# Keeping the high and low halves of every weight block in an HBM scratch

## The chip, the cores and the metric

The kernel runs on one core of one Trainium2 chip. The metric is the device time of one execution in microseconds (us). Five engines work side by side: TensorE (PE; its weight loads are listed as PEld), VectorE (DVE), ScalarE (ACT), GpSimd (POOL) and SyncE (SP), which here issues every DMA from one in-order queue. They are held together by semaphores.

## The reference

One layer of a hybrid decoder runs over a prompt of 2048 tokens and over 8 sample sequences of 8 tokens, with shared weights and D = 1024. In float32, cut to the order of its steps:

```
h = rmsnorm(x);  u = h @ w_in                     # [conf_val | conf_gate | q k v | z | beta | a]
conf = swish(layernorm(dwconv31(val * sigmoid(gate))))
q, k, v = silu(dwconv4(qkv));  q, k = l2norm(q), l2norm(k)
o = gated_delta_rule(q, k, v, g, beta, S);  o = rmsnorm(o) * silu(z)
x = x + concat(conf, o) @ w_out
gate, val = dwconv3(rmsnorm(x) @ w_up)            # 2 x 2816 columns
x = x + (silu(gate) * val) @ w_down
x = x + (p @ w_ple) * sigmoid(x @ w_ple_gate);  y = rmsnorm(x)
```

The states of the convolutions and of the delta rule are outputs too.

## The kernel before

**Number format.** Every large product is made of float32r operands in halves: `hi` is the operand rounded to float32r, `lo` what is left. `gemm` (L269) sums `hi*hi + hi*lo + lo*hi` in one PSUM bank, three matmuls for each of 8 slices of the inner dimension, so a weight block of 1024 x 128 takes 24 matmuls, of 512 columns or of two chunks (256 and 256, in the last pass 256 and 320).

**Passes and phases.** The prompt is cut into four passes of 512 tokens (L1327); the last one carries the 64 sample tokens too. Each pass runs phase b (`w_in`: beta and a, conformer blocks, k, q, v and z, the inverses of triangular blocks, the scan of the delta rule), phase w (`w_out`, residual, norm; its 8 blocks are gone through twice, once for each chunk of tokens), phase f (`w_up` and `w_down`, 22 columns in 11 pairs: four up blocks of a pair, then the product of the pair before with two `w_down` blocks) and phase l (`w_ple_gate`, last norm, output; the norm of the next pass's x runs inside it). A pass uses 114 weight blocks and the small block of beta and a (`ba_weights`, L1284); 106 of the 114 are different.

**The stream of weights.** The blocks are listed in the order of their use (`stream`, L1293 to L1318). `get` (L257) keeps three of them ready: when a block is taken, the one two further on is started. `wblock` (L247) starts one: SP loads 512 KB into a `raw` tile (three buffers), ACT casts it to `whi` (three buffers), and POOL or DVE, as `lo_e` says, subtracts `wlo = raw - whi` (three buffers). A `whi` or `wlo` buffer comes free when TensorE has read the block three back; a `raw` buffer comes free when its split is done. `w_up` and `w_in` blocks are read in runs of 512 bytes, `w_down` blocks in runs of 4 KB. Every block of every pass is loaded and split anew.

**Around it.** In phase f, ACT empties each PSUM bank of an up product twice (`row`, and `y` with the last tap, L1123 to L1125), DVE adds two more taps (`end`, L1127), ACT and POOL split the product of the halves into `fbuf` (L1174), and for the down product DVE adds each bank to the residual `X` (L1149). Three PSUM banks (`g`) serve all the large products. In phase b DVE does the taps of the convolutions, POOL the taps of conformer block 3 (L44) and then the chain of the inverses: blocks go through HBM (`scr`, L760 to L765), 62 operations on POOL write `Tb` (L772 to L777), they come back through `scr2` into `X`, and POOL copies them to `T` (L833), from which TensorE builds the full inverses. In phase w the residual comes back from its scratch `xT` (L1078), 1 MB in runs of 8 KB.

**What sets the order.** The program is written in dependency order, and a scheduler with its own timing model places the instructions on the engines; stretches marked `high_priority` go first. The order on SP is such an order too: a DMA that waits holds back those behind it.

## Time and profile before

| | before |
|---|---|
| median of 3 runs | 3376.66 us (3370.89 to 3382.05) |
| span of the profiled execution | 3377.1 us |
| TensorE busy | 3045.9 us, 90% |
| DVE, POOL, ACT busy | 2285.6, 1932.9, 1480.6 us |
| POOL `wlo` | 362 of 2429 ns |
| DVE `wlo` | 94 of 1403 ns |
| ACT `whi` | 456 of 1051 ns |
| moved by DMA | 295.34 MB, 87 GB/s |

The profiled execution has its span as its own time; it lies 0.4 us above the median of the runs. Busy shares are means over phases with different limits, so the table of stretches and the waits of a phase say more than the page's first line. A stretch's idle time of TensorE is its length less its busy time. In a list of waits the engine that stood still stands first, then what ended the wait. In the chain of waits each piece is what the end of the program waited for at that time. The granted clock is given as a share of TensorE's full speed: 1.00 is its higher level, 2.4 GHz, and a mean below 1 says that a part of the stretch ran at 1.2 GHz.

### The profile page before, as it was taken

What the parts mean: (1) busy time and instruction counts of PE and PEld (TensorE: products, weight loads), DVE (VectorE), ACT (ScalarE), POOL (GpSimd) and SP (SyncE); (2) the same over time, 40 slices, a digit from 0 to 9 for tenths busy, and PEclk for the clock granted to TensorE, in tenths of its full rate; (3) what the DMA queues carried; (4) which work ended last, traced back from release to release, by engine and by line L of the source; (5) the groups of instructions that cost most, each with busy time, mean ns of one, the idle gap of its engine ahead of it and who ended that gap; (6) DMA issues with size and microseconds to landing.
All of it is one profiled execution on the core that took longest, in us unless ns stands there. A gap on an engine that the chain in (4) does not pass through costs nothing. (4 is left out here: it accounts for less than half of the span.)

```text
span 3377.1 us, 48322 instructions
## 1 busy us (share of the span) xinstructions
PE 3045.9 (90%) x17710; PEld 2682.5 (79%) x17710; DVE 2285.6 (68%) x4306; ACT 1480.6 (44%) x2947; POOL 1932.9 (57%) x1987
## 2 busy tenths in 40 slices
PE   7889899999888899998988889999996988999998
PEld 6668777778767877778866877777986878999998
DVE  6999754457898864447698965445796877554555
ACT  4536443344535443334543544334452335443443
POOL 6972555564982455556694455566486404655552
PEclk8999999999989999999998999999997878999999
DMA  4223332233321433233322433233322123222231
GB/s 127 72 57 105 104 106 89 86 96 105 78 69 42 141 106 91 84 100 94 88 72 50 129 97 100 88 93 95 94 59 69 46 79 116 76 76 83 84 90 60
DMA packets 480596, 295.34 MB, mean 87 GB/s; under 512 B 49674, under 2 KB 462859, under 8 KB 479328
## 3 DMA queue, kind: packets, MB, share of 16 engines
q1 hardware_dynamic: 480359, 292.27, 30.1%
q8 instruction: 139, 2.28, 0.3%
q14 instruction: 98, 0.79, 0.1%
HBM read 269.69 MB, written 22.90 MB: 87 GB/s over the span
## 5 line engine op out<-in xcount | busy, mean ns | idle before, releaser
L93 PE MATMUL g<-hT,whi 128*128 128x512 f32 (+2 forms) x5664 | 1519.9, 356 | 60.9 <-ACT t L112 18.9
L109 POOL TENSOR_TENSOR wlo<-raw,whi 128x1024 fp32r<-128x1024 f32 x362 | 877.6, 2429 | 602.4 <-ACT whi L112 567.9
L93 PEld LDWEIGHTS g<-hT,whi 128*128 128x128 f32 x5664 | 1028.5, 196 | 189.7 <-ACT t L112 21.5
L93 PE MATMUL g<-hT,wlo 128*128 128x512 f32 (+2 forms) x2832 | 1001.2, 355 | 8.7 <-POOL wlo L109 8.6
L100 DVE SCALAR_TENSOR_TENSOR y<-row,ffS,y 128x512 f32<-128x512 f32 x352 | 466.0, 1324 | 605.0 <-ACT y L112 601.5
L112 ACT ACTIVATE whi<-raw 128x1024 fp32r<-128x1024 f32 x456 | 475.0, 1051 | 409.8 <-PE g L93 244.6
L93 PEld LDWEIGHTS g<-hT,wlo 128*128 128x128 f32 x2832 | 555.6, 196 | 70.9 <-POOL wlo L109 10.6
L93 PE MATMUL g<-fbuf,whi 128*128 128x512 f32 (+2 forms) x1760 | 474.7, 359 | 64.5 <-DVE X L109 37.4
L93 PEld LDWEIGHTS g<-fbuf,whi 128*128 128x128 f32 x1760 | 305.2, 189 | 134.1 <-DVE X L109 59.5
L109 DVE TENSOR_TENSOR X<-X,g 128x512 f32<-128x512 f32 (+2 forms) x504 | 280.5, 567 | 134.3 <-PE g L93 132.4
L100 DVE SCALAR_TENSOR_TENSOR cacc<-H,cfS,cacc 128x512 f32<-128x512 f32 x352 | 321.4, 928 | 10.4 <-ACT cacc L112 8.5
L93 PE MATMUL g<-fbuf,wlo 128*128 128x512 f32 (+2 forms) x880 | 305.0, 354 | 0.2 <-POOL wlo L109 0.2
L109 POOL TENSOR_TENSOR cacc<-cacc,pr 128x256 f32<-128x256 f32 x224 | 203.9, 932 | 18.4 <-ACT pr L112 17.2
L93 PE MATMUL g<-mx,whi 128*128 128x256 f32 (+1 forms) x1024 | 201.1, 292 | 3.4 <-ACT mx L112 1.4
L112 ACT ACTIVATE fbuf<-y 128x512 fp32r<-128x512 f32 (+1 forms) x88 | 56.8, 645 | 333.3 <-DVE y L109 333.3
L93 PE MATMUL g<-x,whi 128*128 128x256 f32 (+1 forms) x1024 | 197.0, 289 | 0.0
L93 PEld LDWEIGHTS g<-fbuf,wlo 128*128 128x128 f32 x880 | 165.5, 189 | 21.4 <-POOL wlo L109 0.4
L109 POOL TENSOR_TENSOR fbuf<-y,fbuf 128x512 fp32r<-128x512 f32 (+1 forms) x88 | 118.5, 1347 | 108.8 <-ACT fbuf L112 108.8
L93 PEld LDWEIGHTS g<-mx,whi 128*128 128x128 f32 x1024 | 163.0, 192 | 5.6 <-ACT mx L112 2.1
L112 ACT ACTIVATE row<-g 128x512 f32<-128x512 f32 (+1 forms) x292 | 141.7, 485 | 53.0 <-PE g L93 51.2
L93 PEld LDWEIGHTS g<-x,whi 128*128 128x128 f32 x1024 | 164.1, 193 | 0.4
L112 ACT ACTIVATE pr<-H,cfS 128x256 f32<-128x256 f32 x232 | 114.5, 505 | 102.3 <-POOL cacc L109 100.3
(346 smaller groups left out, 4589.4 us busy)
## 6 DMA issues: line engine op xcount, KB each, us to landing
raw<-in_w_up_dram SPq DMA_DIRECT2D x176, 512.0 KB
raw<-in_w_in_dram SPq DMA_DIRECT2D x96, 512.0 KB
raw<-in_w_down_dram SPq DMA_DIRECT2D x88, 512.0 KB
raw<-in_w_out_dram SPq DMA_DIRECT2D x64, 512.0 KB
raw<-in_w_ple_gate_dram SPq DMA_DIRECT2D x32, 512.0 KB
out_dram<-yt SPq DMA_DIRECT2D x16, 512.0 KB
X<-xT SPq DMA_DIRECT2D x7, 1024.0 KB
xt<-in_x_prompt_dram SPq DMA_DIRECT2D x12, 512.0 KB
```

The costliest lines, as they stand in the source:

```text
L93: T.matmul(out, lhsT=lhsT, rhs=rhs, start=start, stop=stop, skip_group_check=skip)
L100: e.scalar_tensor_tensor(out=out, in0=in0, scalar=scalar, in1=in1, op0=op0, op1=op1)
L109: e.tensor_tensor(out=out, in0=a, in1=b, op=op)
L112: A.activation(out, in_, f, **kw)
```

## The change

The first time a block is used, it is loaded and split as before, now into one tile `w` of 8 KB a partition that holds both halves (three buffers in place of three `whi` and three `wlo`, the same space). SP then stores this tile, 1 MB in runs of 8 KB, to a tile of its own in HBM. Each later use, in passes 2 to 4 and in the second round over `w_out` in pass 1, loads the 1 MB from there straight into `w`, with no `raw` tile, no cast and no subtraction. The block of beta and a is treated alike. The diff, without the comments that it drops:

```diff
+    hw = ctx.enter_context(tc.tile_pool(name="hw", bufs=1, space=DRAM))
...
-    def wblock(src, hi_e="a", lo_e="g"):
-        raw = raw_tile("raw")
-        SY.dma_start(raw, src)
-        hi = wp.tile([P, KD, P], F32R, tag="whi", name=nm("whi"), bufs=3)
-        lo = wp.tile([P, KD, P], F32R, tag="wlo", name=nm("wlo"), bufs=3)
-        split(raw, hi, lo, hi_e, lo_e)
-        return hi, lo
+    halves = {}
+
+    def w_tile():
+        return wp.tile([P, 2, KD, P], F32R, tag="w", name=nm("w"), bufs=3)
+
+    def wblock(key, src, hi_e="a", lo_e="g"):
+        w = w_tile()
+        if key in halves:
+            SY.dma_start(w.bitcast(F32), halves[key])
+        else:
+            raw = raw_tile("raw")
+            SY.dma_start(raw, src)
+            split(raw, w[:, 0], w[:, 1], hi_e, lo_e)
+            halves[key] = hw.tile([P, 2, KD, P], F32, tag=nm("halves"), name=nm("halves"))
+            SY.dma_start(halves[key], w.bitcast(F32))
+        return w[:, 0], w[:, 1]
...
     def ba_weights():
+        if "ba" in halves:
+            w = w_tile()
+            SY.dma_start(w[:, 0].bitcast(F32), halves["ba"])
+            return w[:, 0], None
...
-            push(cols(w_in[0], b * P), lo_e=LO[0] if ip else "g")
+            push_cols("in", w_in[0], b * P, lo_e="g")
```

The other calls of `push` get a key (name and column) in the same way.

**ACT, steady part of phase f, pass 2.** The rows are part of one pair; `fbuf` is the split of a finished column, `whi` the cast of a weight block, `row` and `y` empty a bank. Before:

```order
L112 ACTIVATE whi_2252_12956<-raw_2251_12954 128x1024
L112 ACTIVATE row_2249_12921<-g_2250_12923 128x512
L112 ACTIVATE y_2248_12920<-g_2250_12923,ffS_2905 128x512
L112 ACTIVATE y_2248_12920<-y_2248_12920 128x512
L112 ACTIVATE whi_2258_12998<-raw_2257_12996 128x1024
L112 ACTIVATE row_2255_12961<-g_2256_12963 128x512
L112 ACTIVATE y_2254_12960<-g_2256_12963,ffS_2905 128x512
L112 ACTIVATE fbuf_1912_10721<-y_2254_12960 128x512
```

After:

```order
L113 ACTIVATE row_2174_12831<-g_2175_12833 128x512
L113 ACTIVATE y_2173_12830<-g_2175_12833,ffS_2935 128x512
L113 ACTIVATE y_2173_12830<-y_2173_12830 128x512
L113 ACTIVATE row_2178_12867<-g_2179_12869 128x512
L113 ACTIVATE y_2177_12866<-g_2179_12869,ffS_2935 128x512
L113 ACTIVATE fbuf_1917_10627<-y_2177_12866 128x512
```

The casts ahead of `row` are gone; the rest stands in the same order. ACT has 456 casts of weight blocks before and 106 after.

**SP, start of phase w, pass 2.** `X<-xT` is the residual, `pt` an input of phase l, `raw` a block of `w_out`, `w<-halves` a block from the scratch. Before:

```order
L249 DMA raw_1816_10148<-in_w_out_dram 128x8x128 [waits DMAHW7_49,DMAHW4_49,Pool_49]
L1191 DMA pt_2334_13482<-in_p_prompt_dram 128x256 [waits DMAHW0_49,PE_49,Activation_49]
L1078 DMA X_1324_7626<-xT_1116_6484 128x2048 [waits DMAHW1_49,PE_49]
L1191 DMA pt_2336_13489<-in_p_prompt_dram 128x256 [waits PE_49,Activation_49]
L249 DMA raw_1821_10183<-in_w_out_dram 128x8x128 [waits DMAHW5_49,DVE_49]
L249 DMA raw_1826_10218<-in_w_out_dram 128x8x128 [waits DMAHW7_49,DVE_49]
```

After:

```order
L256 DMA w_1839_10015<-halves_603_3052 128x2048 [waits DMAHW5_49,DMAHW0_49,PE_49]
L1204 DMA pt_2209_13128<-in_p_prompt_dram 128x256 [waits DMAHW1_49,PE_49,Activation_49]
L1204 DMA pt_2211_13135<-in_p_prompt_dram 128x256 [waits PE_49,Activation_49]
L1091 DMA X_1409_7692<-xT_1199_6555 128x2048 [waits DVE_49,PE_49]
L256 DMA w_1841_10044<-halves_608_3086 128x2048 [waits DMAHW6_49,PE_49]
L256 DMA w_1844_10075<-halves_614_3122 128x2048 [waits DMAHW7_49,PE_49]
```

The loads waited for POOL or DVE (a split done); now they wait for TensorE (a block read). Before, the block in the first row is number 5 of `w_out`, counted from 0; after it is number 2, and `w_1841` is number 3.

**SP, phase f of pass 1.** Before:

```order
L249 DMA raw_979_5646<-in_w_up_dram 128x8x128 [waits DMAHW6_49,Pool_49]
L249 DMA raw_985_5686<-in_w_up_dram 128x8x128 [waits DMAHW7_49,Pool_49]
L249 DMA raw_991_5728<-in_w_down_dram 128x1024 [waits DMAHW0_49,Pool_49]
L249 DMA raw_997_5768<-in_w_down_dram 128x1024 [waits DMAHW1_49,Pool_49]
L249 DMA raw_1003_5810<-in_w_up_dram 128x8x128 [waits DMAHW2_49,Pool_49]
```

After:

```order
L262 DMA halves_979_5336<-w_976_5331 128x2048 [waits DMAHW2_49,Pool_49]
L259 DMA raw_1000_5453<-in_w_up_dram 128x8x128 [waits DMAHW5_49]
L262 DMA halves_986_5379<-w_983_5374 128x2048 [waits DMAHW4_49,Pool_49]
L259 DMA raw_1007_5494<-in_w_up_dram 128x8x128 [waits DMAHW7_49]
L262 DMA halves_998_5450<-w_995_5445 128x2048 [waits DMAHW6_49,Pool_49]
L259 DMA raw_1014_5537<-in_w_down_dram 128x1024 [waits DMAHW1_49]
```

The wait for POOL has moved from the raw load to the store ahead of it.

## Rows read from the trace of the kernel before

**Rows 1.** The page: span; busy us (share) and instructions of each engine.
```profile
span 3377.1 us, 48322 instructions
...
PE 3045.9 (90%) x17710; PEld 2682.5 (79%) x17710; DVE 2285.6 (68%) x4306; ACT 1480.6 (44%) x2947; POOL 1932.9 (57%) x1987
```

**Rows 2.** Stretches, passes 2 and 4: length, engines' busy us, clock, DMA share, GB/s.
```profile
core 0: us, PE busy (x) PEld busy (x) DVE busy (x) ACT busy (x) POOL busy (x), PEclk, DMA share, GB/s
...
823.20:1072.40 249.20, 216.57 (x1079) 178.79 (x1077) 208.94 (x393) 122.91 (x278) 173.49 (x231) 0.90 0.27 72
1072.40:1139.20 66.80, 60.84 (x492) 58.61 (x493) 62.30 (x178) 38.92 (x90) 27.54 (x19) 1.00 0.45 134
1139.20:1549.30 410.10, 380.26 (x1741) 311.95 (x1740) 221.71 (x293) 165.25 (x253) 234.98 (x186) 0.98 0.32 97
1549.30:1615.80 66.50, 59.38 (x490) 58.32 (x489) 49.85 (x108) 27.70 (x61) 35.08 (x24) 1.00 0.29 79
...
2411.00:2759.20 348.20, 297.47 (x1884) 275.94 (x1883) 270.61 (x630) 139.40 (x354) 187.45 (x256) 0.84 0.25 68
...
2833.50:3297.30 463.80, 449.61 (x3309) 440.03 (x3308) 247.50 (x423) 192.97 (x377) 257.44 (x277) 0.99 0.28 81
```

**Rows 3.** Groups: line, engine, operation, count, busy us, mean ns, idle before.
```profile
L109 POOL TENSOR_TENSOR wlo<-raw,whi 128x1024 fp32r<-128x1024 f32 x362 | 877.6, 2429 | 602.4 <-ACT whi L112 567.9 <-DVE mv L100 7.6 <-DVE rt L109 6.2
...
L109 DVE TENSOR_TENSOR wlo<-raw,whi 128x1024 fp32r<-128x1024 f32 x94 | 131.9, 1403 | 28.1 <-ACT whi L112 21.6 <-POOL X L109 4.2 <-POOL kd L109 2.3
```

**Rows 4.** TensorE's waits, 1236 to 1541 us: total us, times, longest.
```profile
PE g L93 <- DVE X L109: 7.9, 9, 1.6
PE g L93 <- ACT y L112: 7.7, 9, 0.9
```

**Rows 5.** Timeline of a pair, pass 2, three engines: start, us, instruction, idle before.
```profile
1280.50 1.04 ACT L112 ACTIVATE whi<-raw 128x1024 fp32r<-128x1024 f32 x1
...
1282.72 1.82 DVE L100 SCALAR_TENSOR_TENSOR y<-row,ffS,y 128x512 f32<-128x512 f32 x1 [2.80 <-ACT y L112]
...
1285.66 0.74 DVE L100 SCALAR_TENSOR_TENSOR y<-row,ffS,y 128x512 f32<-128x512 f32 x1
...
1282.74 0.73 PE L93 MATMUL g<-fbuf,whi 128*128 128x512 f32 x2 [0.87 <-ACT y L112]
...
1285.20 0.73 PE L93 MATMUL g<-fbuf,whi 128*128 128x512 f32 x2 [0.79 <-DVE X L109]
```

**Rows 6.** Stretches: one pair of phase f, one block of phase w.
```profile
1300.07:1334.96 34.89, 33.22 (x145) 26.86 (x144) 16.77 (x19) 13.17 (x18) 20.42 (x17) 1.00 0.30 91
...
1110.92:1113.81 2.89, 2.89 (x27) 2.89 (x26) 2.85 (x7) 1.48 (x2) 1.37 (x1) 1.00 0.67 199
```

**Rows 7.** Chain of waits, phases b and w of pass 4: start, us, piece.
```profile
2455.52 1.05 ACT whi L112
2456.60 1.91 DVE wlo L109
...
2466.28 1.23 DVE wlo L109
...
2634.23 1.07 ACT whi L112
2635.37 3.73 POOL wlo L109
...
2773.57 1.16 DVE wlo L109
...
2795.99 1.13 DVE wlo L109
```

**Rows 8.** Residual load: its issue, then DMA share in 40 slices of 276 to 282.
```profile
276.46 0.36 SPq L1078 DMA_DIRECT2D X<-xT  x1
...
DMA  0000000009970924569697979999995100000000
...
q1 hardware_dynamic: 144, 1.05, 49.7%
```

**Rows 9.** DMA queue, 1110 to 1139.2 us: packets, MB, share of 16 engines.
```profile
q1 hardware_dynamic: 8082, 4.08, 48.2%
```

More of the change, by code (lines that the diff above doesn't have):

```diff
@@ L1281, in push_down @@
         for j in range(2):
-            push(w_down[0, (g0 + j) * P:(g0 + j + 1) * P, :].rearrange("p (k c) -> p k c", c=P))
+            push(("down", g0 + j), w_down[0, (g0 + j) * P:(g0 + j + 1) * P, :].rearrange("p (k c) -> p k c", c=P))
     def ba_weights():
+        if "ba" in halves:
+            w = w_tile()
+            SY.dma_start(w[:, 0].bitcast(F32), halves["ba"])
+            return w[:, 0], None
         baw = dp.tile([P, KD, 8], F32, tag="baw", name=nm("baw"), bufs=1)
         SY.dma_start(baw, w_in[0].rearrange("(k p) c -> p k c", p=P)[:, :, 3072:3080])
-        bah = wp.tile([P, KD, P], F32R, tag="whi", name=nm("bah"), bufs=3)
+        bah = w_tile()[:, 0]
         G.memset(bah.bitcast(F32), 0.0)
@@ L1290, in ba_weights @@
         tt(V, bah[:, :, 8:16], baw, bah[:, :, 0:8].bitcast(F32), SUB)
+        halves["ba"] = hw.tile([P, KD, P], F32, tag="halves_ba", name="halves_ba")
+        SY.dma_start(halves["ba"], bah.bitcast(F32))
         return bah, None
@@ L1295, in step_kernel @@
         for b in PRE_K:
-            push(cols(w_in[0], b * P), lo_e=LO[0] if ip else "g")
-            push(cols(w_in[0], CW + b * P), lo_e=LO[0] if ip else "g")
+            push_cols("in", w_in[0], b * P, lo_e="g")
+            push_cols("in", w_in[0], CW + b * P, lo_e="g")
         for j in range(4, 8):
-            push(cols(w_in[0], D + j * P))
+            push_cols("in", w_in[0], D + j * P)
         for b in POST_K:
-            push(cols(w_in[0], b * P), lo_e=LO[0])
-            push(cols(w_in[0], CW + b * P), lo_e=LO[0])
+            push_cols("in", w_in[0], b * P, lo_e=LO[0])
+            push_cols("in", w_in[0], CW + b * P, lo_e=LO[0])
         for j in (0, 1, 2, 3, 8, 9, 10, 11):
-            push(cols(w_in[0], D + j * P), lo_e=LO[1] if j < 4 else LO[2])
+            push_cols("in", w_in[0], D + j * P, lo_e=LO[1] if j < 4 else LO[2])
         for h in range(H):
-            push(cols(w_in[0], 2560 + h * P), lo_e=LO[3])
+            push_cols("in", w_in[0], 2560 + h * P, lo_e=LO[3])
         for _ in range(2):
             for ob in range(KD):
-                push(cols(w_out[0], ob * P), lo_e="v" if ob % 2 else "g")
+                push_cols("out", w_out[0], ob * P, lo_e="v" if ob % 2 else "g")
         for g0 in range(0, FT, 2):
             for f in (g0, g0 + 1):
-                push(cols(w_up[0], f * P))
-                push(cols(w_up[0], (FT + f) * P))
+                push_cols("up", w_up[0], f * P)
+                push_cols("up", w_up[0], (FT + f) * P)
             if g0:
@@ L1317, in step_kernel @@
         for ob in range(KD):
-            push(cols(w_ple_gate[0], ob * P))
+            push_cols("ple", w_ple_gate[0], ob * P)
     ps_ = [make_pass(ip) for ip in range(NPASS)]
```

6 lines of the change are left out of this document (4 added, 2 removed).

## The prediction

> **What bounds the kernel now.** I read the page's busy times first. TensorE is busy 90% of the span, DVE 68%, POOL 57% [rows 1]; the DMA engines are busy 0.27 to 0.45 of a stretch [rows 2]. So the splits of the weights, which run on ACT, POOL and DVE, are beside the main work, and what they cost must be looked for in the 331 us in which TensorE stands still (3377.1 − 3045.9). Next the table by stretch [rows 2], cut at the stage borders of pass 2 and at some of pass 4: TensorE idles 249.20 − 216.57 = 32.6 us in phase b of pass 2, 6.0 in phase w, 29.8 in phase f, 7.1 in phase l; 50.7 in phase b of pass 4, 14.2 in its phase f. Pass 3 repeats pass 2. Together the idle time of passes 2 to 4 is some 230 us. That is all that the change can give back there, apart from TensorE's clock: granted at 0.90 in phase b of pass 2 and 0.84 in pass 4, so part of it ran at the lower level (1.2 GHz), against 1.00 in phase w.
>
> Then who ends the idle time. In the steady part of phase f there are just two waits a pair of columns, nine times each, 15.6 us in all [rows 4]. The timeline of one pair [rows 5] tells what is behind both. ACT makes a `whi` (1.04 us) before it empties the last PSUM bank of the up product, and TensorE waits 0.87 us for that bank. DVE's first tap takes 1.82 us with POOL in a `wlo`, and 0.74 us without one, so the addition behind it comes late and TensorE waits another 0.79 us. In phase b I read the chain of waits of pass 4 [rows 7]: it goes through DVE and the POOL chain of the inverses, and seven `whi` and three `wlo` pieces are on it; in phase w of that pass four `wlo` on DVE are.
>
> **Part by part.** *Splits removed.* 350 of 456 blocks lose ACT's cast and the subtraction, 2.43 us on POOL or 1.40 us on DVE [rows 3]. Most of that is cover already, so I count only what ended a wait.
>
> Phase f, passes 2 and 3: both waits of a pair go, since ACT has no `whi` ahead of the bank (the order of ACT shows it) and DVE's tap falls from 1.82 to 0.74 us. 15.6 us in nine pairs, and about 1.4 for the two other pairs: −17 a pass, −34. What is next there is TensorE itself: 33.22 busy of 34.89 us a pair [rows 6], so no more than 1.7 a pair can come. In pass 4 blocks are wider and only 14.2 us are idle; the same cause holds for about a third: −4.
>
> Phase b: in pass 4 the pieces on the chain are seven `whi` of 0.94 to 1.07 us, 7.2 together, and `wlo` of 1.91, 1.23 and 3.73, 6.9 together [rows 7]: 14 us. Behind them the next chain waits, so I take 12, and 10 in passes 2 and 3, which have the same 24 blocks but no sample group: −32. The ends: nothing, if the POOL chain of the inverses sets the end by itself, and 25 a pass, if DVE does (rival 1). TensorE's new order speaks for caution: 40 of the 106 small products of the inverses stand behind the last weight product of pass 2, where 10 stood before.
>
> Phase l: 7.1 us idle, ended by DVE beside POOL and ACT splits. I take −3 in passes 2 and 3, −1 in pass 4.
>
> *Loads added.* A block comes as 1 MB instead of 512 KB, into the slot that TensorE reads, so it is asked for only when the block three back is finished. Before, raw tiles were up to three blocks further ahead. The nearest row is the residual's load from its scratch: the same form, 128 runs of 8 KB [rows 8]. Its data moves until 4.3 us after the issue (slices of 0.15 us from 276.0); I estimate 5.0 with its completion. It takes 49.7% of 6 us of the 16 engines, 2.98 us. A block of 24 products takes 5.5 us at 512 columns (33.22 us for the six blocks of a pair) and 2.89 us at 256 [rows 6]; the times up to the due time that follow are TensorE's new order, counted in these.
> Phase f: the worst case of a pair is the second up block, whose slot comes free three products before the down product ends: 0.7 + 5.5 = 6.2 us until it is read, against 5.0. Nothing is lost, with 1.2 us to spare. The others have 7 to 11 us.
> Phase w: TensorE starts three blocks together and finishes them after the scan, so block 3 is asked for some 1.4 us of products before it is due: a wait of 5.0 − 1.4 = 3.6 us. From there each load has 5.4 to 5.9 us and one follows every 2.89 us where each takes 2.98: up to 0.1 each for 12, and the residual's own 1 MB lies among them. Against this stand DVE's `wlo` that go (four of 1.13 to 1.16 us on the chain of pass 4, [rows 7]). Net I take +1.5 a pass, +4; the ends are −5 and +8 a pass.
> The Trainium skill, page HBM Reference, section Specifications (TRN2), says that a core streaming alone measures about 425 GB/s. By that a block would move in 2.5 us, loads would keep up with 2.89 us, phase w would lose 1 us a pass less and the sum would be 3311. The one load in the trace measured 2.98 us, and I keep that.
> Phases f and l also begin with a block that is asked for 3.0 and 3.6 us before it is due: 2 and 1.5 us lost. The first is set against the waits for ACT that go at the same place; the second costs +4 in all.
>
> *Stores added, pass 1.* 106 stores of 1 MB stand in SP's queue, each waiting for a split. Behind each stands the raw load three blocks on, and that one already waited for the same split, since it needs the raw buffer (the order of SP shows the pairs). So the new wait holds nothing back, and the issue itself (0.36 us) is hidden. The DMA engines take more: raw 1.73 us a block (48.2% of 29.2 us for 4.08 MB, [rows 9], is 3.45 us a MB) plus 2.98 is 4.7 of 5.5 us. They fit, but each small transfer of the inverses' chain may lie behind a store. Three such hops of 2 us: +6; the ends are 0 and +15. The second round over `w_out` in this pass also loads ready halves, which I count as nothing: it trades a split for a load.
>
> Sum: −34 − 4 − 32 − 7 + 4 + 4 + 6 = −63. The profiled span is 3377.1 us, and the median of the runs 3376.66, so the two can be taken as one: 3314 us.
>
> **Rival 1: phase b gains much more.** DVE is busy 208.94 of 249.20 us there [rows 2]. Sixteen of its 24 splits ran on DVE: 16 × 1.40 = 22 us. If DVE sets the pace, these come in full, and with less idle time TensorE stays at its higher level longer: 0.90 granted means about a fifth of the stretch at half speed, and half of that loss is some 12 us. Then −34 a pass instead of −11, 3314 − 69 = 3245. For it: DVE was at 84%, and POOL stops slowing it. Against it: the chain of pass 4 runs mostly through POOL, whose steps stay. The Trainium skill, page SBUF — State Buffer, section Who interferes with whom, says of DVE and POOL that the second of two contending instructions waits for the whole of the first. Of that 1.82 against 0.74 us shows a part (1.08 of POOL's 2.4 us); by the full rule rival 1 would be likelier.
>
> **Rival 2: slower, the loads come late.** One mechanism: a 1 MB load or store takes longer than the one measured, because reads, stores and raw loads share the same engines. With S for its engine time and 2.0 + S for landing, phase w loses 13 × (S − 2.89) a pass, a pair of phase f loses S − 4.2, and the 66 blocks of phase f of pass 1 lose 1.73 + S − 5.5 each. At S = 4.1 that is 47 + 0 + 22 = 69 us in three passes and one, as much as the gain; it decides from there. At S = 4.5 it is 63 + 10 + 48 = 121: 3435. For it: no two such transfers overlap in the trace. Against it: 2.98 measured, and raw loads in runs of 512 bytes, streaming, make 3.45 a MB.
>
> **Rival 3: no change.** The waits in phase f go, but phase b comes out later by as much: 30 more products of the inverses run behind the weights, at some 1 us each with their copies, in each of passes 2 and 3, 60 in all: 3374. That the change doesn't do what it says can be left out: ACT's order has 106 casts of weights after, 456 before.
>
> **How the numbers follow.** Forecast 0.57, rival 1 0.17, rival 2 0.14, rival 3 0.12. The likeliest time is 3314, by its own bounds 3285 to 3350. The range of 8 in 10 takes in rival 1, rival 3 and the near end of rival 2: 3240 to 3385. A measurement can tell about 0.3%, 10 us, from no change: faster than that 0.73 (the forecast and rival 1), within it 0.12, slower 0.15.
>
> **What would show it.** In the profile after: ACT's casts x106; no wait of TensorE for ACT `y` or DVE `X` in the steady part of phase f, and pairs of 33.2 us; DMA share near 0.8 in phase f of pass 1 and 0.5 to 0.6 in the others; waits of TensorE for a load at the start of phase w, about 3.6 us, none in a pair. Phase b of passes 2 and 3 at 239 us. I am wrong if waits for loads appear in every pair or every block of phase w (rival 2), if phase b falls under 225 (rival 1) or stays above 249 (rival 3).

## The result and the profile after

The changed kernel takes 3235.18 us (median; 3230.47 to 3239.94) against 3379.25 of the kernel before beside it: 0.9578 of its time, with a 95% interval of 0.9562 to 0.9594. The profiled span is 3238.2 us after and 3377.1 before, 139 us less. The forecast was 63 us less.

The page of after, span and busy us of each engine (compare [rows 1]):

```profile
span 3238.2 us, 47390 instructions
PE 3006.7 (93%) x17710; PEld 2685.9 (83%) x17710; DVE 1890.8 (58%) x4227; ACT 1165.6 (36%) x2594; POOL 1169.1 (36%) x1710
```

POOL lost 764 us of work, DVE 395 and ACT 315. TensorE's idle time fell from 331 to 231.5 us, and its busy time by 39. Stretches of after, the columns as in [rows 2]: phases b and w of pass 1; phase f of pass 1; b and w of pass 2; phase f of pass 2; one pair of it; phase l; b and w of pass 4.

```profile
0.00:375.20 375.20, 307.76 (x1712) 266.55 (x1713) 285.89 (x625) 166.33 (x387) 212.13 (x292) 0.85 0.59 187
430.90:756.40 325.50, 322.01 (x1436) 265.51 (x1435) 167.70 (x221) 136.21 (x195) 207.11 (x156) 1.00 0.87 289
823.40:1129.40 306.00, 269.87 (x1565) 234.94 (x1564) 221.61 (x544) 127.47 (x328) 141.71 (x234) 0.93 0.45 158
1184.70:1507.40 322.70, 321.11 (x1435) 265.74 (x1435) 133.46 (x221) 81.98 (x138) 48.77 (x97) 1.00 0.53 194
1270.13:1302.77 32.64, 32.64 (x145) 27.03 (x144) 12.46 (x18) 7.61 (x12) 4.56 (x10) 1.00 0.52 195
1507.40:1567.00 59.60, 59.29 (x496) 58.87 (x495) 40.06 (x114) 21.15 (x52) 17.72 (x16) 1.00 0.50 175
2311.90:2707.40 395.50, 350.05 (x2348) 328.94 (x2347) 283.83 (x780) 144.14 (x402) 157.95 (x257) 0.88 0.40 136
```

Phases f and l of pass 2 have no idle time left to speak of, and a pair takes 32.64 us with TensorE busy throughout. The same stretches of the kernel before, where [rows 2] and [rows 6] don't have them (b and w of pass 1; phase f of pass 1; b and w of pass 2; of pass 4):

```profile
0.00:345.00 345.00, 288.06 (x1712) 248.58 (x1712) 291.69 (x619) 170.33 (x388) 221.53 (x292) 0.93 0.33 91
408.10:755.40 347.30, 327.37 (x1436) 264.23 (x1435) 180.76 (x223) 135.56 (x196) 201.01 (x157) 1.00 0.32 96
823.40:1139.30 315.90, 277.32 (x1571) 237.30 (x1570) 271.13 (x570) 161.93 (x367) 201.12 (x250) 0.92 0.31 85
2411.20:2833.70 422.50, 363.16 (x2353) 339.10 (x2353) 338.75 (x811) 182.17 (x443) 217.34 (x275) 0.86 0.28 77
```

Phases b and w must be taken together: after, the products of the first three blocks of `w_out` lie between 1043 and 1085 us, among those of the scan, so the border between the phases has moved. Cut at the first product of each phase, the 139 us lie here ("start of f" is the stretch up to the first down product):

| change in us | predicted | pass 1 | pass 2 | pass 3 | pass 4 |
|---|---|---|---|---|---|
| b and w | pass 1: +6; −8.5, −8.5, −10.5 | +30.2 | −10.0 | −9.1 | −27.0 |
| start of f | 0 | −7.3 | −8.3 | −8.0 | −1.5 |
| rest of f | pass 1: 0; −17, −17, −4 | −21.8 | −23.8 | −23.9 | −10.7 |
| l | −1.5, −1.5, +0.5 in passes 2 to 4 | −0.9 | −6.9 | −9.2 | −0.3 |

The surprise is pass 1. It splits every block once, as before (the second round over `w_out` apart), and stores 106 blocks of 1 MB on top, its phases b and w are 30 us longer, and still it comes out level: the rest of its phase f is 22 us shorter. Something other than the removed work acts there. The timeline of ACT in phase f of pass 1, before and after (columns as in [rows 5]):

```profile
538.43 1.06 ACT L112 ACTIVATE whi<-raw 128x1024 fp32r<-128x1024 f32 x1 [4.16 <-POOL wlo L109]
539.40 0.58 ACT L112 ACTIVATE row<-g 128x512 f32<-128x512 f32 x1
539.88 0.77 ACT L112 ACTIVATE y<-g,ffS 128x512 f32<-128x512 f32 x1
```

After:

```profile
553.18 0.60 ACT L113 ACTIVATE row<-g 128x512 f32<-128x512 f32 x1 [4.11 <-PE g L94]
553.68 0.77 ACT L113 ACTIVATE y<-g,ffS 128x512 f32<-128x512 f32 x1
554.34 1.06 ACT L113 ACTIVATE w<-raw 128x1024 fp32r<-128x1024 f32 x1
```

Before, the cast stands ahead of `row` and `y`, and the prediction put the wait of 0.87 us down to that; after, it stands behind them. So the order changed where the split stayed. The tile `w` is the likeliest cause, and the first experiments test it.

### The profile page after: what moved, and what is told of

Same layout as the page of the kernel before. It is cut to its first block, busy times and chain, and to the rows that moved or that the text cites. A ratio compares the mean times of both kernels' runs of the same rounds, so it can differ in the third digit from the quotient of the medians.

```text
span 3238.2 us, 47390 instructions
## 1 busy us (share of the span) xinstructions
PE 3006.7 (93%) x17710; PEld 2685.9 (83%) x17710; DVE 1890.8 (58%) x4227; ACT 1165.6 (36%) x2594; POOL 1169.1 (36%) x1710
## 4 chain that ended last, share of the span: by engine, by line
PE 70%; POOL 12%; DVE 9%; DMA 5%; ACT 2%; issue 2%; SPq 0%; ACTq 0%; DVEq 0%; POOLq 0%
PE g L94 61%; POOL Tb L110 6%; PE d L94 4%; PE m L94 3%; DMA w<-halves 3%; POOL cacc L110 2%; PE d L98 2%; DVE h L101 1%; PE m L98 1%; DVE rt L110 1%; DVE H L101 1%; DVE cacc L101 1%; DVE y L101 1%; POOL X L110 0%; POOL T L846 0%
## 5 line engine op out<-in xcount | busy, mean ns | idle before, releaser
L94 PE MATMUL g<-hT,w 128*128 128x512 f32 (+2 forms) x8592 | 1674.5, 354 | 72.3 <-DMA w<-halves 22.4
L94 PEld LDWEIGHTS g<-hT,w 128*128 128x128 f32 x8592 | 1423.8, 195 | 260.9 <-issue 29.5
L101 DVE SCALAR_TENSOR_TENSOR y<-row,ffS,y 128x512 f32<-128x512 f32 x352 | 268.1, 763 | 696.3 <-ACT y L113 692.3
L94 PE MATMUL g<-fbuf,w 128*128 128x512 f32 (+2 forms) x2640 | 520.0, 354 | 9.7 <-DMA w<-halves 5.4
L94 PEld LDWEIGHTS g<-fbuf,w 128*128 128x128 f32 x2640 | 437.4, 188 | 75.9 <-DVE X L110 8.6
L110 POOL TENSOR_TENSOR w<-raw,w 128x1024 fp32r<-128x1024 f32 x88 | 231.4, 2634 | 144.2 <-ACT w L113 122.1
L94 PE MATMUL g<-mx,w 128*128 128x256 f32 (+1 forms) x1536 | 213.8, 297 | 14.2 <-DMA w<-halves 13.0
L94 PEld LDWEIGHTS g<-mx,w 128*128 128x128 f32 x1536 | 201.2, 198 | 18.4 <-DMA w<-halves 14.8
L94 PE MATMUL g<-x,w 128*128 128x256 f32 (+1 forms) x1536 | 202.5, 288 | 0.0
L94 PEld LDWEIGHTS g<-x,w 128*128 128x128 f32 x1536 | 195.9, 193 | 0.3
```

The source lines that it names most:

```text
L94: T.matmul(out, lhsT=lhsT, rhs=rhs, start=start, stop=stop, skip_group_check=skip)
L101: e.scalar_tensor_tensor(out=out, in0=in0, scalar=scalar, in1=in1, op0=op0, op1=op1)
L110: e.tensor_tensor(out=out, in0=a, in1=b, op=op)
```

## Experiments

Medians and ratios are against the runs of the kernel before beside them; the other columns are stretches of the profiled run in us, cut as above, "f" with its start. The kernel that the diffs start from is the changed one unless said otherwise.

| kernel | median, ratio (95% interval) | b+w of pass 1 | f of 1 | b+w of 2, 3 | f of 2, 3 | l of 2, 3 | b+w, f of 4 |
|---|---|---|---|---|---|---|---|
| before | 1 | 345 | 410 | 316, 315 | 410, 410 | 66, 70 | 423, 464 |
| changed | 3235.2, 0.9578 | 375 | 381 | 306, 306 | 378, 378 | 60, 61 | 395, 451 |
| merged_only | 3340.5, 0.988 (0.9859–0.990) | 351 | 392 | 319, 322 | 389, 384 | 67, 70 | 428, 469 |
| last_hi | 3326.8, 0.9849 (0.9834–0.9864) | 351 | 384 | 318, 318 | 389, 390 | 67, 70 | 427, 468 |
| two_tiles | 3258.7, 0.9649 (0.9622–0.9676) | 356 | 408 | 309, 304 | 378, 377 | 59, 60 | 404, 453 |
| two_swap | 3239.0, 0.9582 (0.956–0.9604) | 364 | 382 | 305, 311 | 378, 380 | 59, 60 | 399, 452 |
| no_reuse | 3334.9, 0.9865 (0.9843–0.9887) | 363 | 387 | 321, 316 | 385, 386 | 67, 70 | 423, 468 |
| ffn_only | 3301.6, 0.9765 (0.9743–0.9787) | 352 | 392 | 320, 323 | 380, 379 | 67, 70 | 425, 452 |
| mix_only | 3255.8, 0.9631 (0.9607–0.9655) | 374 | 381 | 307, 306 | 381, 383 | 59, 61 | 398, 464 |
| no_out | 3244.0, 0.960 (0.9584–0.9617) | 356 | 384 | 311, 311 | 377, 377 | 59, 60 | 403, 451 |
| idle_splits | 3321.8, 0.9829 (0.9815–0.9844) | 371 | 381 | 355, 310 | 379, 378 | 59, 60 | 427, 454 |
| idle_again | 3291.9, 0.9741 (0.9713–0.977) | 368 | 381 | 326, 319 | 379, 376 | 59, 61 | 428, 452 |
| idle_dve | 3237.7, 0.958 (0.9548–0.9612) | 375 | 381 | 305, 300 | 376, 377 | 59, 61 | 409, 452 |
| idle_rest | 3271.5, 0.9681 (0.9653–0.971) | 370 | 381 | 313, 322 | 379, 379 | 60, 61 | 409, 457 |
| scr_pool | 3241.4, 0.959 (0.9571–0.961) | 368 | 379 | 307, 305 | 378, 376 | 59, 60 | 403, 450 |
| four_bufs | 3202.5, 0.948 (0.9466–0.9494) | 369 | 381 | 302, 301 | 370, 370 | 60, 61 | 400, 447 |
| four_late | 3206.3, 0.9489 (0.9468–0.951) | 364 | 382 | 302, 302 | 370, 370 | 60, 61 | 400, 449 |
| four_swap | 3194.5, 0.9454 (0.9436–0.9473) | 363 | 379 | 304, 301 | 370, 370 | 59, 60 | 396, 447 |

Phases b and w vary from one execution to the next. In pass 1, TensorE, DVE, ACT and POOL run the same instructions in the same order in seven of these kernels (the changed one, mix_only, idle_splits, idle_again, idle_dve, idle_rest, four_bufs), and the stretch takes from 375.2 down to 367.6 us at a granted clock of 0.85 to 0.88. The shortest, of idle_again (columns as in [rows 2]):

```profile
0.00:367.60 367.60, 300.79 (x1711) 260.67 (x1712) 285.62 (x625) 166.07 (x387) 212.09 (x292) 0.87 0.60 191
```

Differences of up to some 8 us in such a stretch are therefore not read; an edit that also moves the order can add to them. The stretches of phase f are steadier: the same seven lie within 0.4 us in the start of f of pass 1, and agree to 0.1 us in the rest of it.

### Is it the work removed, or the tile?

**merged_only**: the kernel before with the tile `w` alone.

```diff
-        hi = wp.tile([P, KD, P], F32R, tag="whi", name=nm("whi"), bufs=3)
-        lo = wp.tile([P, KD, P], F32R, tag="wlo", name=nm("wlo"), bufs=3)
-        split(raw, hi, lo, hi_e, lo_e)
+        w = wp.tile([P, 2, KD, P], F32R, tag="w", name=nm("w"), bufs=3)
+        split(raw, w[:, 0], w[:, 1], hi_e, lo_e)
```

> The kernel before with one edit: the two tiles whi and wlo of a block become one tile w with both halves (three buffers). Nothing is stored, every block of every pass is still loaded raw and split. Theory A (order): what made phase f shorter is the place of ACT's cast, behind row and y of the block that just ended instead of ahead of them; the merged tile alone brings this order, since it comes free with the last product of a block, as the bank does. Then phase f (from the first down product) is 325 us in passes 1 to 3 instead of 347, 384 instead of 395 in pass 4, the first pair of phase f about 7 us shorter, and the whole about 3377 - 3*22 - 11 - 3*7 = 3279 us, up to 15 less or more by phase b. Theory B (work removed): phase f got shorter because the casts and subtractions are gone. Then this kernel stays at 347 us a pass in phase f and at 3377 us +- 10 in all, and the 22 us of pass 1 came from the stores' effect on the order.

It takes 0.988 of the time before. From the first down product on, phase f is 327, 326 and 327 us in passes 1 to 3 instead of 347. TensorE's waits in phase f of pass 2 (total us, times, longest), beside the two of [rows 4]:

```profile
PE g L94 <- DVE X L110: 2.2, 2, 1.9
```

So with all 456 splits in place the two waits are gone. Theory A holds there for passes 1 to 3. The whole is 61 us above A's 3279: the rest of phase f in pass 4 is 6 us longer instead of 11 shorter, the start of f is shorter in pass 3 alone (7 us), and phases b and w are 22 us longer over the four passes.

**last_hi**: the kernel before, two lines of `gemm` exchanged.

```diff
-            mm(ps, whi(k), mlo(k), False, False, skip=False)
-            mm(ps, wlo(k), mhi(k), False, k == nk - 1, skip=False)
+            mm(ps, wlo(k), mhi(k), False, False, skip=False)
+            mm(ps, whi(k), mlo(k), False, k == nk - 1, skip=False)
```

> The kernel before with two lines of gemm exchanged: of the three products of a slice, lo*hi now comes second and hi*lo last. Nothing else changes: separate whi and wlo tiles, every block split, no scratch. In the kernel before, the last product of a block reads wlo, so whi comes free one product (0.23 us) before the bank is finished, and ACT's cast goes ahead of row and y. With the exchange whi comes free with the bank, and the order of ACT shows the cast behind row and y. Theory A1 (the place of the cast is what counts, and the release of whi sets it): phase f from the first down product on is 325 to 328 us in passes 1 to 3 as in merged_only, 347 before; the whole 3315 to 3345 us. Rival (the merged tile helped in another way): phase f stays at 347 us and the whole at 3378 +- 10.

It takes 0.9849 of the time before, 50 us less, for two lines. Phase f from the first down product on is 325, 326 and 326 us. ACT's order in pass 2, and all that is left of TensorE's waits in its steady pairs:

```profile
1306.10 0.60 ACT L112 ACTIVATE row<-g 128x512 f32<-128x512 f32 x1 [4.11 <-PE g L93]
1306.59 0.77 ACT L112 ACTIVATE y<-g,ffS 128x512 f32<-128x512 f32 x1
1307.26 1.06 ACT L112 ACTIVATE whi<-raw 128x1024 fp32r<-128x1024 f32 x1
```
```profile
PE g L93 <- DVE X L109: 1.2, 1, 1.2
```

This settles what the tile does in passes 1 to 3: in the kernel before, `whi` comes free one product ahead of the bank, the scheduler puts the cast first, and `row` and `y` wait behind 1.04 us of it. Released together with the bank, the cast goes last. In pass 4 neither kernel gains.

**two_tiles**: the changed kernel with the tile taken apart again.

```diff
-        w = w_tile()
+        w = w_tile(), w_tile("wlo")
         if key in halves:
-            SY.dma_start(w.bitcast(F32), halves[key])
+            for i in range(2):
+                SY.dma_start(w[i].bitcast(F32), halves[key][:, i])
```

> The changed kernel, but the halves of a block lie in two tiles whi and wlo as in the kernel before, stored and loaded by two transfers of 512 KB each; the scratch is used as in the changed kernel. This takes the merged tile away from the change. Theory: removing the splits is enough by itself where they are removed, so phase f of passes 2 and 3 stays at 321 to 325 us and of pass 4 at 384, while in pass 1, which splits, it goes back to 345 to 348 us; b, w and l within 8 us a pass of the changed kernel; the whole 3250 to 3275 us. Rival: without the merged tile phase f is at 345 us or more in the other passes too, and the whole is 3310 us or more.

3258.7 us. From the first down product on, phase f is 346.0 us in pass 1, and 322.5 and 321.6 in passes 2 and 3. TensorE's waits in phase f of pass 1:

```profile
PE g L94 <- DVE X L110: 7.9, 9, 1.6
PE g L94 <- ACT y L113: 7.7, 9, 0.9
```

These are [rows 4] to the tenth. So the removal alone would have brought phase f of passes 2 and 3, as the prediction says; the tile brings pass 1. In passes 2 and 3 either cause alone takes most of the waits away (merged_only 326 and 327 us, two_tiles 322), so what they are worth doesn't add up.

### What each part of the scratch is worth

**no_reuse** stores in pass 1 and never loads; **ffn_only** and **mix_only** use the scratch for one half of the blocks each; **no_out** for all but `w_out`.

The first edit is that of no_reuse, the second that of ffn_only; mix_only has `"in", "out", "ple"` in this place, no_out `"in", "up", "down", "ple"`.

```diff
-        if key in halves:
+        if False:
```
```diff
-            halves[key] = hw.tile([P, 2, KD, P], F32, tag=nm("halves"), name=nm("halves"))
-            SY.dma_start(halves[key], w.bitcast(F32))
+            if key[0] in ("up", "down"):
+                halves[key] = hw.tile([P, 2, KD, P], F32, tag=nm("halves"), name=nm("halves"))
+                SY.dma_start(halves[key], w.bitcast(F32))
```

> The changed kernel, but nothing is loaded from the scratch: pass 1 stores the halves, passes 2 to 4 (and the second round over w_out in pass 1) load raw and split again. Against merged_only it prices the 106 stores. Theory S (stores cost): phases b and w of pass 1 take 375 us as in the changed kernel, 30 more than in the kernel before, and no_reuse is 25 to 30 us slower than merged_only. Theory R (reloads cost): the loss of pass 1 comes from the second round over w_out, whose loads wait for their stores (6.4 us once), and from the order; then no_reuse is within 10 us of merged_only. By theory A of merged_only passes 2 to 4 are as in that kernel; by theory B they are as in the kernel before.

> The changed kernel with the scratch for the up and down blocks alone (66 stores in pass 1, 198 loads); the blocks of w_in, w_out and the gate and the block of beta and a are split anew in every pass. If the gain adds up by phases, phases f keep theirs against before (22 + 7 us in pass 1, 24 + 8 in passes 2 and 3, 11 + 2 in pass 4: 106 us) and phases b, w and l of passes 2 to 4 fall back to the kernel before; without stores in phases b and w pass 1 loses its 30 us: 3377 - 106 = 3271 us. By theory A (order alone) ffn_only is within 10 us of merged_only; by theory B it is about 100 us faster than merged_only.

> The changed kernel with the scratch for w_in, beta and a, w_out and the gate alone (40 stores and the small one, 152 loads); up and down blocks are split anew in every pass. Theory A: phase f is 325 us in passes 1 to 3 all the same, and only what the halves bring in phases b, w and l separates it from merged_only: -10, -9 and -27 us in b and w of passes 2 to 4, -7 and -9 in l, +30 in pass 1: about 22 us faster than merged_only, near 3240 to 3260 us. Theory B: phase f at 347 us a pass, 3377 + 30 - 46 - 16 = 3345 us.

> The changed kernel, but the blocks of w_out are loaded raw and split in all eight rounds; all other blocks go through the scratch. It prices the ready halves in phase w, where TensorE starts them while the scan runs. If my reading of phase w holds (waits for loads and splits saved about cancel): b and w together within 6 us of the changed kernel in passes 2 and 3, and pass 1 6 to 10 us faster since its second round no longer waits for its own stores: 3220 to 3235 us. Rival: the splits of w_out delay the scan through DVE, b and w are 10 us or more longer a pass, and the whole is 3250 to 3265 us.

no_reuse against merged_only: pass 1 takes 816.8 us against 810.1, 6.7 more with the stores, and the totals are equal within their intervals, so theory S (25 to 30 us) falls. The changed kernel, which adds the loads in the second round over `w_out`, takes 823.4 there, another 6.6. Both differences are no larger than what separates executions of one order. ffn_only misses its 3271 by 31 us: its phases f give 92 us of the 106, and its phases b and w, which should have been as before, are 20 us longer over the four passes, as in merged_only. mix_only lies in theory A's range. mix_only keeps all splits of phase f and yet has it at 327 us from the first down product on, as merged_only. Loading the up and down blocks ready-made brings −3 to −5 us more there in each of passes 2 and 3 and −13 to −15 in pass 4 (ffn_only against merged_only, the changed kernel against mix_only). The larger part of the scratch's gain is in phases b, w and l. no_out (0.960, interval from 0.9584) can't be told from the changed kernel (0.9578, interval to 0.9594), and its median lies between both expectations. Its pass 1 is 18 us shorter, as read; its phases b and w there are 12 to 19 us shorter than in the seven executions of one order. What b and w of passes 2 to 4 lost (5, 5 and 8) is not read.

### Engine time or path in phase b

**idle_splits** does the casts and subtractions of `w_in` in passes 2 to 4 all the same, on tiles that nothing reads. **idle_again** lets them read the block just loaded (`src` is its high half, `ih` and `idle[2]` spare tiles); **idle_dve** has DVE's subtractions alone, **idle_rest** the casts and POOL's subtractions.

```diff
             SY.dma_start(w.bitcast(F32), halves[key])
+            if key[0] == "in":
...
+                act(ih, src)
+                tt(G if lo_e == "g" else V, idle[2].bitcast(F32R), src, ih.bitcast(F32), SUB)
```

> The changed kernel, and for each of the 24 w_in blocks of passes 2 to 4 the cast on ACT and the subtraction on DVE or POOL are done all the same, on three tiles that nothing else uses and whose result nothing reads: the engines' work is back, the weights don't wait for it. Phase b of passes 2 and 3 is 246 us in merged_only and 220 in the changed kernel, 355 and 330 in pass 4. Theory E (engine time: the work of the splits, on DVE above all, sets the pace of phase b): it goes back to 240 us or more in passes 2 and 3 and the whole to 3285 to 3310 us. Theory P (path: a weight block no longer waits for load, cast and subtraction one behind the other): it stays at 225 us or less, the whole within 12 us of the changed kernel's 3235.

The scheduler did 46 casts in pass 2, none in pass 3 and 21 in pass 4, and b and w grew by 49, 4 and 31 us. It speaks for engine time, but at an uneven dose, so:

> As idle_splits, but each idle cast and subtraction reads the block that has just been loaded, so that the scheduler can't pile those of pass 3 into pass 2, as it did there (46 casts in pass 2, none in pass 3, 21 in pass 4): now 24 casts on ACT, 16 subtractions on DVE and 8 on POOL in each of passes 2 to 4. There, phases b and w together grew by 49 us with 46 splits, by 4 with none and by 31 with 21. Theory E (engine time sets the pace of phase b): some 1.07 us for each split, 22 to 28 us in b and w of passes 2 and 3 and 28 to 36 in pass 4, the whole 3305 to 3325 us. Theory P (the path of the weights does): below 5 us a pass, the whole under 3250; the 49 us were the double dose alone.

> The changed kernel with only DVE's part of the idle work: 16 subtractions in phase b of each of passes 2 to 4, no cast, nothing on POOL. If DVE alone sets the pace (rival 1 of the prediction, 16 * 1.40 = 22 us), b and w grow by 16 to 22 us a pass and the whole to 3285 to 3305 us, nearly as much as idle_again. If it is POOL, ACT or their contention with DVE, b and w grow by under 8 us a pass and the whole stays below 3260.

> The other part: 24 casts on ACT and 8 subtractions on POOL in phase b of each of passes 2 to 4, nothing on DVE. If DVE alone sets the pace, b and w grow by under 5 us a pass and the whole stays within 12 us of 3235. If POOL (8 * 2.43 = 19 us a pass ahead of or between the steps of the inverses) or ACT sets it, they grow by 10 to 20 us a pass, the whole to 3265 to 3295, and idle_dve stays low. If the two parts add up to idle_again's growth, no single engine sets the pace.

In pass 4 these kernels also put two tiles of the sample group (`cst`, `win`) on the idle tiles, a dependence that the changed kernel doesn't have and that no run prices. Phases b and w of pass 3 (306.00 us in the changed kernel, DVE busy 221.38, POOL 142.30), in idle_again, idle_dve and idle_rest, one row each:

```profile
1579.40:1898.30 318.90, 277.60 (x1564) 237.74 (x1563) 255.60 (x560) 149.30 (x352) 172.73 (x242) 0.92 0.43 152
```
```profile
1563.20:1863.70 300.50, 270.36 (x1564) 232.28 (x1563) 241.75 (x561) 127.49 (x328) 152.19 (x234) 0.95 0.46 161
```
```profile
1569.30:1890.90 321.60, 281.65 (x1563) 242.55 (x1563) 236.02 (x545) 148.79 (x352) 166.61 (x242) 0.90 0.44 151
```

With all the work back, b and w grow by 20, 13 and 33 us in passes 2, 3 and 4, and the whole by 57 us. merged_only, which has the whole path too, lies 13, 16 and 33 above the changed kernel. So the engines' time explains the gain; the path need not be called on, and theory P falls. One thing in idle_again is not engine time alone: its idle work reads `w`, so a few loads on SP wait for it (5 times, 15.5 us, in pass 3). TensorE's waits for loads didn't grow by that, and idle_splits, whose idle work reads no `w`, grew by 49 us for 46 splits in pass 2, no less for each. The sizes of theory E were too high in passes 2 and 3 (22 to 28 expected). DVE's 16 subtractions alone change nothing in passes 2 and 3 (DVE busy 241.75 of 300.50 us), cost 13 us in pass 4, and leave the whole as it was (3237.7), so rival 1's mechanism falls: DVE's busy share was not the bound. ACT and POOL alone give 7, 16 and 14, and 36 us in all. The two parts make 39 of the 57 us by the medians; whether the rest is more than noise, and how ACT, POOL and DVE share in the pace, stays open. In idle_rest DVE is busy 236.02 us, 15 more than in the changed kernel, with no instruction more to do: eight of its instructions beside the eight subtractions on POOL take 13.9 us longer than in the changed kernel (below).

### What bounds the changed kernel, and a better one

TensorE's longest wait in phase b of pass 2 is for a load, 9.3 us. SP's timeline there shows why: the load stands behind a store of `Tb`, which stands 21.6 us waiting for POOL.

```profile
PE g L94 <- DMA w<-halves: 9.3, 1, 9.3
```
```profile
970.55 1.68 SPq L793 DMA_DIRECT2D scr<-Tb  x2
972.32 2.05 SPq L256 DMA_DIRECT2D w<-halves  x1
```
```profile
SPq L793 <- POOL row L511: 21.6, 1, 21.6
```

**scr_pool** issues the transfers of `scr2` from POOL's queue; **four_bufs** gives passes 2 to 4 a fourth weight buffer, in the space of two raw tiles, and asks one block earlier.

```diff
-            SY.dma_start(Tc[b * B:(b + 1) * B], scr2[b].rearrange("q i f c -> i q (f c)"))
+            G.dma_start(Tc[b * B:(b + 1) * B], scr2[b].rearrange("q i f c -> i q (f c)"))
```
```diff
+        if ip and not turn_of(0, 4):
+            return spare("w4", F32R)
...
-        while len(ready) < 3 and stream:
+        while stream and len(ready) < (4 if stream[0][0] else 3):
```

The first is one of scr_pool's lines, the two stores of `Tb` are changed alike; in four_bufs an entry of `stream` begins with its pass, counted from 0.

> The changed kernel with one edit: the six transfers of the inverses around scr2 (two stores of Tb, four loads into X) are issued from POOL's queue instead of SP's. In the changed kernel the store of Tb waits on SP for POOL's chain for 21.6 us, a load of a weight block stands behind it, and TensorE then waits 9.35 us for that load in pass 2 and 9.24 in pass 3. Theory Q (the queue holds the load back): both waits fall below 3 us, phase b of passes 2 and 3 by 6 to 12 us each, the whole by 12 to 25 us to about 3215. Rival (the inverses set the end of phase b anyway, or POOL's own issue is slower): the wait goes, but phase b stays within 4 us and the whole within 8 us of 3235.

> The changed kernel with a fourth buffer for weight blocks in passes 2 to 4, in the space that two of the three raw tiles leave free after pass 1, so that a load is asked for one block earlier. TensorE waits for a load of halves 40.9 us in 16 waits in the changed kernel, 34 of them in passes 2 to 4. Theory L (lead: loads are asked for too late): those fall below 12 us and the whole by 20 to 35 us to about 3208. Rival (what stands next in the queue takes their place: the scan, the copies of the inverses, the store of Tb ahead of the load): the waits for loads fall, but the whole gains under 10 us.

scr_pool: the wait for the load is gone, and the time is the same (3241.4). TensorE's longest wait in b and w of pass 2 is now this one, which had been 0.8 us:

```profile
PE d L98 <- POOL T L846: 10.0, 2, 9.2
```

The wait moved to the inverses, as its rival said. four_bufs gains 33 us, at the upper end of theory L, and no wait for a load is left in passes 2 to 4, where there were 14 of 34 us. What can be read of the gain is 21 us in phases f: in the start (−6 each in passes 2 and 3) and the rest (−2, −2, −5). The other pieces are no larger than the differences between executions: b and w of passes 2 to 4 (−4, −5, +5), and 6 us in pass 1, where there is no fourth buffer and phases b and w keep their order. In b and w of pass 2 the wait for the load went to the inverses again, as in scr_pool:

```profile
PE d L98 <- POOL T L863: 11.3, 2, 10.5
```

Phase f of pass 2 is then TensorE alone:

```profile
1169.00:1489.50 320.50, 320.50 (x1435) 265.99 (x1434) 134.02 (x221) 82.10 (x138) 49.57 (x97) 1.00 0.55 196
```

**four_late** is four_bufs and stores `w_out` in its second round of pass 1 only; **two_swap** is two_tiles with the exchange of last_hi; **four_swap** adds the fourth buffer to that.

```diff
-                push_cols("out", w_out[0], ob * P, lo_e="v" if ob % 2 else "g")
+                push_cols("out", w_out[0], ob * P, keep=r == 1, lo_e="v" if ob % 2 else "g")
```

> The version that the runs so far point to: four_bufs (fourth buffer in passes 2 to 4, 3202.5 us), and in pass 1 the blocks of w_out are stored in the second of their two rounds, which splits them anew and so doesn't wait for loads of what was just stored. In four_bufs that wait is 6.3 us, and no_out, which neither stores nor loads w_out, was 18 us faster than the changed kernel in pass 1. Theory: pass 1 is 6 to 15 us shorter than in four_bufs and passes 2 to 4 as there: 3187 to 3197 us. Rival: the splits of the second round cost what the wait did, and it is within 5 us of 3202.

> two_tiles (halves in two tiles, two transfers a block, scratch used throughout) with the exchange of last_hi. Pass 1: phase f falls from 346 to 325 us by the exchange. For phases b and w of pass 1, 375 us in the changed kernel, 356 in two_tiles, 351 in merged_only and last_hi, 362 in no_reuse, theory M (the merged tile, which is free only when the last half is read and ready only when both are stored, costs pass 1 its 20 us): they stay at 350 to 360 us, and the whole is 3225 to 3240 us. Rival (the order that comes with the late release costs them): they go back to 368 us or more, and the whole is 3245 us or more.

> Two tiles, the exchange, and the fourth buffer of four_bufs in passes 2 to 4. If pass 1 of two_swap and passes 2 to 4 of four_bufs come together: pass 1 about 805 us, passes 2 to 4 as in four_bufs, the whole 3185 to 3200 us, against 3202.5 of four_bufs. Rival: the two transfers a block and two issues on SP cost in passes 2 to 4 what pass 1 gains, 3200 us or more.

four_late is equal to four_bufs within their intervals, as its rival said; that the splits cost what the wait did is not shown beyond that. two_swap has phase f of pass 1 at 324.9 us from the first down product on, and the changed kernel's time; its b and w of pass 1 are 364 us, between both theories, so that question stays open. four_swap is the fastest, 3194.5 us, 0.9454 of the kernel before (0.9436 to 0.9473), within its theory's range.

## Why the prediction was wrong

The sign and the mechanism of phase f in passes 2 and 3 were right, the size was not: 3314 us forecast, 3240 the low end, 3235 measured. What failed is the size of several terms, and a term put at nothing (the tile `w`). Of the 76 us between −63 and −139, the start of f holds 18, phases b and w of pass 4 16, phase f of passes 2 and 3 14, phase l 13, phase f of pass 4 7, pass 1 6 and phases b and w of passes 2 and 3 2. By the prediction's own terms:

- **Phase f, passes 2 and 3 (−34; measured −47.7).** The waits went, for the reason given (two_tiles). The size failed at "no more than 1.7 a pair can come". I took 33.22 us busy in [rows 6] as the floor. Away from waits three products follow every 0.68 us, so a block of 24 takes 5.44 and six of them 32.64, and that is what a pair takes now: 2.25 come. A busy time next to a wait holds more: the last product before it stands with its whole modelled 0.39 us, where the next product otherwise starts after 0.23, and the first two after it take 0.73 us [rows 5], where two take 0.62 otherwise. For two waits that is 0.54 of the 0.58 us. TensorE in the kernel before, pass 2:

```profile
1277.63 0.61 PE L93 MATMUL g<-hT,whi 128*128 128x512 f32 x2
1278.09 0.39 PE L93 MATMUL g<-hT,wlo 128*128 128x512 f32 x1
1278.31 0.61 PE L93 MATMUL g<-hT,whi 128*128 128x512 f32 x2
```

- **Pass 1 (+6; measured 0).** The stores' +6 fits the 6.7 us of no_reuse, which is no larger than the differences between executions, so it is not confirmed. Two terms were missing. The tile `w` was costed at nothing, as "the same space"; its release changed ACT's order, and I had looked at that order in pass 2 only, where the casts are gone. That is worth −22 us. The −7 in the start of f are not the tile's: that stretch takes 63.1 us before, 64.8 in merged_only and ffn_only, 55.8 in mix_only and 55.7 in the changed kernel. Against it, phases b and w lost 30 in the profiled execution, 23 to 30 over the seven of the same order. In steps these are 6 in merged_only, 18 in no_reuse with the stores, 30 with the reloads of `w_out`, which I had counted as nothing; without `w_out` in the scratch (no_out) 11 are left. But two_tiles, which stores and reloads too, lost 11 only (13 up to the last product of `w_out`), so the steps are no sum of causes. The granted clock shows where the time is: 0.85 against 0.93, so by these rows some 112 us at the lower level against 48 (375.2 × 0.15 × 2, 345 × 0.07 × 2), and TensorE busy 19.7 us longer for the same 1712 products. The rest of the 30 is idle time. How it divides between tile, order, stores and reloads stays open; two_swap didn't settle it.
- **Phase f, pass 4 (−4; −10.7).** Here the tile brings nothing (merged_only +6, with nine waits for DVE's `X` of 12.4 us in all); the removal alone brings 9 (two_tiles), and beside the tile 15 (ffn_only against merged_only). I had taken a third of 14.2 us of idle time. From the first down product on, idle time fell by 5 us, and busy time by another 5 that I had not counted, as in a pair.
- **Start of f (0; −17.8 in passes 2 to 4).** I set the late load (2 us; it was 3.9 in pass 2) against the waits for ACT (5.3, of which 0.7 is left there). Three waits behind DVE, 4.3 us, went as well, and TensorE was busy 3.3 us less at a granted clock of 0.94 instead of 0.89.
- **Phase l (−3 net; −16.4).** Its 7.1 us of idle time went whole, and I had taken 3. The load that I priced at 1.5 a pass cost nothing there; a wait of 1.4 us for a load stands in the last down product instead.
- **Phases b and w, passes 2 and 3 (−17; −19.1).** The sum held, by the wrong reasoning: I priced pieces of the chain of pass 4, and idle_again shows that the engines' time is what counted; that the sum came out is luck, and each pass's part is little more than the 8 us that are not read. In pass 4 the same step gave −10.5 and −27.0 came: merged_only, with all the splits, takes 33 us more there (and so does idle_again, with its added dependence), so the 12 us that I took from the pieces on one chain were about a third of it. My caution about the inverses behind the last weight product was not needed.
- **Loads.** In phase w 2.1 us in four waits came, where I had 3.6 and up to 1.2. I had no load on the list in phase b, and the longest wait of all is there, behind the store of `Tb`. A block of 1 MB (1.05 million bytes) takes little else than the 2.98 us I kept: phase f of pass 2 moves 194 GB/s at a share of 0.53, or 2.87 us of the 16 engines for a block; phase f of pass 1, with its raw loads and stores, 289 at 0.87, or 3.16. By the 425 GB/s of the page HBM Reference of the Trainium skill, section Specifications (TRN2), the estimate is about 2.5; the first of the two rows lies between that and mine. Landing took longer than my 5.0 in places: pieces of 7.2 and 7.4 us in the chain of waits of pass 2, the first right behind the two stores of `Tb`, the second in a row of loads behind the residual's.

```profile
972.32 7.18 DMA w<-halves
...
1093.88 7.39 DMA w<-halves
```

Rival 1 came nearest in time (3245), but idle_dve takes its reason away. Its sign, phase b under 225 us, did come out (219.7 up to the first product of `w_out`), but only because that border moved. Rival 2's price of 4.1 us a MB was not reached, and rival 3's tail did not come. What would have changed the forecast was in reach: compare ACT's order in pass 1 too, and take the pair's floor from the products' own pace.

## What to carry to other kernels

A buffer's last reader can decide where its refill stands in the order of the engine that fills it: before building a scratch, look whether a cast stands ahead of the emptying of a PSUM bank, and which product releases it; here two exchanged lines alone gave 50 us, where the whole change gave 144. Price removed side work by putting it back idle rather than by its pieces on the chain of waits. Once loads replace computed operands, look at their lead: here a fourth buffer took away every wait for a load in passes 2 to 4 and was worth 33 us, of which 21 in phases f can be read.

## What the runs showed of the hardware

Where DVE's first tap, which reads two tiles, starts while POOL is in a long subtraction, it waits for all that is left of it. From the timelines, before and after, in phase f of pass 1 (DVE's first tap and POOL's `wlo`; then DVE's product of the halves and POOL's `w`):

```profile
557.36 2.37 POOL L109 TENSOR_TENSOR wlo<-raw,whi 128x1024 fp32r<-128x1024 f32 x1 [1.38 <-ACT whi L112]
...
558.47 1.81 DVE L100 SCALAR_TENSOR_TENSOR y<-row,ffS,y 128x512 f32<-128x512 f32 x1 [2.80 <-ACT y L112]
```
```profile
561.38 2.81 POOL L110 TENSOR_TENSOR w<-raw,w 128x1024 fp32r<-128x1024 f32 x1 [1.45 <-ACT w L113]
...
561.96 2.77 DVE L110 TENSOR_TENSOR y<-y,y 128x512 f32<-128x512 f32 x1
```

The ends: POOL 559.73 and DVE 560.28; POOL 564.19 and DVE 564.73. In the phases f of the kernel before, 169 such taps start at least half a microsecond before a subtraction ends; they all end 0.544 to 0.556 us after it, and alone they take 0.74. Not every DVE instruction waits: 14 additions of a PSUM bank to `X`, which read one tile and a bank, start in such a subtraction and end before it. The prediction read 1.82 against 0.74 as a part of such a wait. It was the whole of what was left: the page SBUF — State Buffer of the Trainium skill, section Who interferes with whom, says that a DVE instruction with two SBUF inputs contends with a GpSimd instruction that reads SBUF, and calls the contention an exclusive lock, and the trace agrees. In pass 1 after, the same blocking (2.77 us) falls on an instruction that TensorE's list of waits in the steady pairs doesn't name.

The clock can differ where the order doesn't. Over phases b and w of pass 1 the same instructions in the same order were granted 0.85 in three executions and 0.87 to 0.88 in four, with TensorE busy 307 to 308 us in the former and 300 to 303 in the latter.
